# Hybrid attention and convolution layer, one core: buffer slots handed out in order of release, seven attention operations per head from VectorE to ScalarE, other operand places in the output projection, earlier residual loads

## The chip, the cores and the metric

One core of one Trainium2 chip. The time is device microseconds (us) of one launch. The engines are PE (TensorE: matmuls and transposes), DVE (VectorE), ACT (ScalarE), POOL (GpSimd) and SP (SyncE, which here only issues DMAs). Each engine runs its own instructions in program order; semaphores join them.

## The reference

One layer, 512 positions behind 16 learned meta tokens, width 2048. A root-mean-square norm, one projection into all groups, a gated linear attention group (4 heads) and a short gated convolution group (8 blocks), one output projection, a second norm and the residual:

```python
xn = rmsnorm(h, g_pre)
q, k, v, z_gla, r, hc, gate_b, gate_c, z_conv = split(xn @ w_in)
log_a = log_sigmoid(r @ w_gate_up + b_gate) / 16
o = gla_chunked(q * 128 ** -0.5, k, v, log_a)   # S_t = diag(exp(log_a)) S_{t-1} + k^T v, o_t = q_t S_t
y_gla = rmsnorm(o, g_gla_out) * silu(z_gla)
y_conv = gate_b * causal_dwconv(gate_c * hc, w_conv) * silu(z_conv)
out = h + rmsnorm(concat(y_gla, y_conv) @ w_out, g_post)
```

## The kernel before, in words

**Products.** Every fp32 matmul is made of three: operands are split into a high part (`hi`) and a low part (`lo`), and hi·hi, hi·lo and lo·hi are summed. A pair of weight tiles (a `Pair`, named after its two tiles: z2z3, k1q1, v2v3, z4z5, k2q2, v4v5, z6z7, k3q3, v6v7, then h0c0, b0s0 to b7s7) goes by a Strassen scheme of seven products P5, P1, P6, P2, P3, P7, P4 instead of eight; P2 adds into the PSUM bank of P1, P3 into that of P5. The operands of the activations stand ready split in the tiles xa, xb and xt. One product is 24 matmuls.

**What a product needs.** Its weight block comes by a DMA of 512 KB into a slot named `raw` (five slots, named by their blocks "11", "12", "21", "22"). For five of the seven products DVE first adds or subtracts two blocks in place (`add`, L188, or L219 for P7). Then `split` makes the two halves: ACT casts `whi` (L123) and DVE subtracts to `wlo` (L124), three buffers each. Two products are prepared ahead of the one that PE works on.

**What leaves a product.** `away` copies PSUM to `f` and `q` on ACT (P5 and P1: L259, L262) and combines on DVE (u, v and the destination: L264, L252, L276). f, q, u, v lie in the pool `ev`, which is opened after the pool `ini` of the start is closed and takes its memory; in `ini` lie first xr (the activations) and then rstd and tt.

**Attention between products.** The stages of each head are generators of which a few steps run after each product: decay (`decay`), scores and state (`gla_b`, `gla_c`), output (`gla_d`, `gla_e`). In `decay` of a head ACT takes the absolute value (L856), Exp (L860) and Ln (L861), each of the last two behind a load of its activation table; DVE makes min(z + b, 0) (L857), subtracts the logarithm (L862), scans (L863) and goes on with L869 to L878. `gla_c` copies the first state from PSUM on DVE (L947), `gla_d` scales the output rows on DVE (L972).

**The end.** `Whole` makes the first quarter of the output projection by plain products, `Out` the other three by the seven-product scheme, in two halves each, with the operand blocks of y (11, 21, 12, 22 and the sums S1 to S4) split into places in xa, xb and xt by `y_blocks`. In the last half (`self.end`) the order is P1, P5, P6, P3, P2, P7, P4. After P3 `rest` closes the pool of xa, opens one for the residual rows in its place, and SP loads them (4 DMAs of 1 MB, L531). Then DVE ends the rows (`finish`, L556), and SP and ACT store them (L559), 16 DMAs of 256 KB.

**Order.** The program is written in the order of the loops, and a scheduler places each engine's instructions; so an instruction can stand elsewhere on its engine than the text of the kernel has it.

## Time and profile before

| | |
|---|---|
| median of 3 runs | 829.04 us (827.64 to 830.21) |
| the profiled execution | 829.95 us |
| its span from the first to the last instruction | 827.5 us |
| PE busy | 795.5 us (96%) |
| DVE busy | 698.5 us (84%) |
| ACT busy | 428.5 us (52%) |
| POOL busy | 2.3 us |
| DMA | 98.97 MB, mean 120 GB/s |

Times below are microseconds from the start of the span unless ns is written. A row of a timeline gives an instruction's start and length, and in brackets how long its engine stood idle before it and what released it. PE's own idle time in the span is short, so every view starts from PE and asks what released each of its waits.

### The profile page before, as it was taken

Reading aid. Unit: us, or ns where it says so; the run is one execution under the profiler, and the core shown is the slowest. Engines: PE = TensorE matmul, PEld = TensorE weight load, DVE = VectorE, ACT = ScalarE, POOL = GpSimd, SP = SyncE. Lnnn points to the kernel's source line nnn. Section 1 sums busy time; section 2 is a strip of 40 time slices with the busy share of each in tenths; the row PEclk is TensorE's granted clock in tenths of the full one; section 3 lists DMA queues with packets and bytes.
Section 4 is the critical chain, followed back from the end, with each engine's and each line's share of the span. In section 5 each row is a group of like instructions: output and inputs, shape, how many; then the busy total and the mean of one; then the engine's idle time right before and its main releaser. Section 6 shows DMA issues by size and latency. Waiting matters only on the chain.

```text
span 827.5 us, 15174 instructions
## 1 busy us (share of the span) xinstructions
PE 795.5 (96%) x6364; PEld 777.6 (94%) x6364; DVE 698.5 (84%) x848; ACT 428.5 (52%) x610; POOL 2.3 (0%) x14
## 2 busy tenths in 40 slices
...
GB/s 278 229 51 68 112 128 102 78 116 132 84 96 110 179 64 81 86 229 103 103 102 103 102 105 106 120 102 122 106 111 122 181 77 75 104 101 106 101 61 346
DMA packets 34052, 98.97 MB, mean 120 GB/s; under 512 B 4064, under 2 KB 8800, under 8 KB 33344
## 3 DMA queue, kind: packets, MB, share of 16 engines
...
## 4 chain that ended last, share of the span: by engine, by line
PE 80%; DVE 10%; ACT 4%; issue 3%; DMA 2%; DVEq 0%; SPq 0%; ACTq 0%
PE out L63 5%; PE out3P L63 4%; PE out1P L63 4%; PE out2P L63 3%; PE v L63 3%; PE v6v7P L63 3%; PE k2q2P L63 2%; PE h0c0P L63 2%; PE k3q3P L63 2%; PE v2v3P L63 2%; PE b0s0P L63 2%; PE h1c1P L63 2%; PE h7c7P L63 2%; PE h6c6P L63 2%; PE h5c5P L63 2%
## 5 line engine op out<-in xcount | busy, mean ns | idle before, releaser
L123 ACT CAST whi<-raw 128x1024 fp32r<-128x1024 f32 x225 | 235.5, 1051 | 274.9 <-DVE raw L188 89.0
L124 DVE TENSOR_TENSOR wlo<-raw,whi 128x1024 fp32r<-128x1024 f32 x225 | 273.7, 1220 | 61.5 <-ACT whi L123 58.9
L188 DVE TENSOR_TENSOR raw<-raw 128x1024 f32<-128x1024 f32 x75 | 90.4, 1220 | 8.2 <-DMA raw<-in_w_t_dram 7.2
L219 DVE TENSOR_TENSOR raw<-raw 128x1024 f32<-128x1024 f32 x25 | 30.5, 1221 | 0.5
L134 ACT CAST whi<-raw 128x1024 fp32r<-128x1024 f32 (+2 forms) x13 | 10.9, 845 | 19.6 <-PE v L63 12.8
L63 PE MATMUL out<-whi,xt 128*128 128x512 f32 x64 | 20.0, 394 | 0.0
L63 PE MATMUL out2P<-whi,xt 128*128 128x256 f32 x96 | 17.4, 282 | 0.4 <-ACT whi L123 0.4
L63 PE MATMUL out3P<-whi,xt 128*128 128x256 f32 x96 | 17.4, 282 | 0.4 <-ACT whi L123 0.4
L63 PE MATMUL out1P<-whi,xt 128*128 128x256 f32 x96 | 17.3, 281 | 0.0
L63 PEld LDWEIGHTS out3P<-whi,xt 128*128 128x128 f32 x96 | 14.7, 188 | 0.6 <-ACT whi L123 0.6
L63 PEld LDWEIGHTS out2P<-whi,xt 128*128 128x128 f32 x96 | 14.7, 188 | 0.6 <-ACT whi L123 0.6
L63 PEld LDWEIGHTS out1P<-whi,xt 128*128 128x128 f32 x96 | 14.8, 188 | 0.1
L63 PEld LDWEIGHTS out<-whi,xt 128*128 128x128 f32 x64 | 12.0, 188 | 2.7
L63 PE MATMUL out3P<-wlo,xt 128*128 128x256 f32 x48 | 13.5, 281 | 0.0
L63 PE MATMUL out1P<-wlo,xt 128*128 128x256 f32 x48 | 13.5, 281 | 0.0
L63 PE MATMUL out2P<-wlo,xt 128*128 128x256 f32 x48 | 13.5, 281 | 0.0
L63 PE MATMUL out<-wlo,xt 128*128 128x512 f32 x32 | 12.6, 394 | 0.0
L135 DVE TENSOR_TENSOR wlo<-raw,whi 128x1024 fp32r<-128x1024 f32 (+2 forms) x13 | 12.5, 968 | 0.0
L593 DVE SCALAR_TENSOR_TENSOR y<-hh,wc,y 128x512 f32<-128x512 f32 x16 | 12.0, 748 | 0.2
L347 ACT ACTIVATE junk<-y 128x256 f32<-128x256 f32 x18 | 7.5, 418 | 8.7 <-DVE y L465 8.4
L658 DVE SCALAR_TENSOR_TENSOR xa<-xr,gp,xa 128x528 fp32r<-128x528 f32 x8 | 5.9, 762 | 6.9 <-ACT xa L657 6.9
L63 PE MATMUL out2P<-whi,xa 128*128 128x256 f32 x64 | 11.7, 283 | 0.0
...
## 6 DMA issues: line engine op xcount, KB each, us to landing
raw<-in_w_t_dram SPq DMA_DIRECT2D x108, 512.0 KB, 4.3
...
raw<-in_w_o_dram SPq DMA_DIRECT2D x16, 256.0 KB, 3.9
...
z<-zd SPq DMA_DIRECT2D x8, 256.0 KB, 3.0
yd<-z SPq DMA_DIRECT2D x8, 256.0 KB, 2.8
...
```

The lines of the kernel that those rows point to most:

```text
L63: nc.tensor.matmul(out_, lhsT, rhs, start=start, stop=stop, **kw)
L123: A.copy(hi, raw)
L124: V.tensor_tensor(out=lo, in0=raw, in1=hi.bitcast(F32), op=ALU.subtract)
L134: A.copy(hi[:, k, :], raw[:, k, :])
L135: V.tensor_tensor(out=lo[:, k, :], in0=raw[:, k, :], in1=hi[:, k, :].bitcast(F32), op=ALU.subtract)
L188: V.tensor_tensor(out=a, in0=a, in1=b, op=ALU.add)
L219: V.tensor_tensor(out=raw["11"], in0=raw["11"], in1=raw["22"], op=ALU.subtract)
L347: A.activation(junk, oy["src"], AF.Square, accum_out=fin["ssq"][:, t, n:n + 1])
L593: V.scalar_tensor_tensor(out=y, in0=hh[:, i:i + S], scalar=wc[:, j, i:i + 1], in1=y, op0=ALU.mult, op1=ALU.add)
L658: V.scalar_tensor_tensor(out=xt[1][:, :, xk, :], in0=src, scalar=gp[:, kt:kt + 1], in1=xt[0][:, :, xk, :].bitcast(F32), op0=ALU.mult, op1= ...
```

## The change

- **Slots.** `new_raw` takes one of five named slots from a list, and `free` puts a slot back where its last reader is written; `load_free` starts the next load of one list `loads` whenever a slot is in the list. Before, each pair loaded its own blocks and, after some products, those of the next pair.
- **Attention on ACT.** In `decay` relu(−z − b) on ACT (L874 after, with a negated bias nbg that POOL makes once) replaces DVE's min(z + b, 0); the sign goes into the next operation (L880 after, a fused multiply and subtract in place of a subtraction). Exp and Ln stand before two yields instead of after one. `gla_c`'s copy and `gla_d`'s four scalings go from DVE to ACT (L965, L990 after).
- **`ini`.** tt is allocated first, ahead of xr and rstd.
- **Operands of y.** 21 and S4 lie in the third part of xt, 11 and S1 in xa, S2 in xb.
- **The end.** `rest` runs after P5 instead of P3 of the last half; the small square root that sets up the table is written there instead of in `Whole`.

```diff
+    slots = [f"raw{i}" for i in range(5)]
+    held = {}
     def new_raw(shape=None):
-        return wp.tile(shape or [P, NB, P], F32, tag="raw", name="raw", bufs=5)
+        tag = slots.pop(0)
+        t = wp.tile(shape or [P, NB, P], F32, tag=tag, name="raw", bufs=1)
+        held[id(t)] = (t, tag)
+        return t
+    def free(t):
+        slots.append(held.pop(id(t))[1])
...
     class Pair:
-        def prepare(self, name, nxt):
-            for b in ("21", "22", "11", "12"):
-                self.load(b)
+        blocks = ("21", "22", "11", "12")
+        def prepare(self, name):
...
-            if nxt and name in ("P5", "P6", "P4"):
-                nxt.load({"P5": "21", "P6": "22", "P4": "11"}[name])
-                if name == "P4":
-                    nxt.load("12")
+            if name in ("P6", "P3", "P7", "P4"):
+                free(raw[{"P6": "21", "P3": "12", "P7": "11", "P4": "22"}[name]])
...
+    def load_free():
+        while slots and loads:
+            p, b = loads.pop(0)
+            p.load(b)
     def prepare_next():
-        n = len(ready)
-        p, name, last = line[n]
-        after = [q for q, _, _ in line[n:n + 9] if q is not p]
-        ready.append(p.prepare(name, after[0] if after else None))
+        p, name, last = line[len(ready)]
+        load_free()
+        ready.append(p.prepare(name))
+        load_free()
...
-        for b, two, s in (("11", xt, 2), ("21", xa, 0), ("12", xt, 1), ("22", xb, 0)):
+        for b, two, s in (("21", xt, 2), ("11", xa, 0), ("12", xt, 1), ("22", xb, 0)):
...
-        for name, two, s, b, c in (("S1", xb, 1, "22", "21"), ("S3", xt, 0, "21", "11"),
-                                   ("S2", xa, 1, "11", "22"), ("S4", xa, 0, "12", "11")):
+        for name, two, s, b, c in (("S1", xa, 1, "22", "21"), ("S3", xt, 0, "21", "11"),
+                                   ("S2", xb, 1, "11", "22"), ("S4", xt, 2, "12", "11")):
...
             if name == "P1":
                 A.copy(q, pt)
+                if self.end:
+                    A.activation(small.tile([P, 1], F32, name="sqrt_eps2"), epst, AF.Sqrt)
             elif name == "P5":
                 A.copy(f, pt)
+                if self.end:
+                    rest()
...
                 self.put(0, 1, pt, w, sub)
-                if self.end:
-                    rest()
...
     with tc.tile_pool(name="ini", bufs=1, reuse_waits="tile") as ini:
+        tt = ini.tile([P, NB, XHALF], F32, name="tt")
         xr = ini.tile([P, KT, L], F32, name="xr")
...
             A.activation(a[:, t], zp[:, 0:XHALF], AF.Abs, bias=bg[:, h:h + 1])
-            V.tensor_scalar(out=Bc[:, t], in0=zp[:, 0:XHALF], scalar1=bg[:, h:h + 1],
-                            scalar2=0.0, op0=ALU.add, op1=ALU.min)
-        yield
+            A.activation(Bc[:, t], zp[:, 0:XHALF], AF.Relu, bias=nbg[:, h:h + 1], scale=-1.0)
         A.activation(a, a, AF.Exp, scale=-1.0)
         A.activation(a, a, AF.Ln, bias=1.0)
-        V.tensor_tensor(out=a, in0=Bc, in1=a, op=ALU.subtract)
+        yield
+        yield
+        V.scalar_tensor_tensor(out=a, in0=Bc, scalar=-1.0, in1=a, op0=ALU.mult, op1=ALU.subtract)
...
-        V.tensor_copy(stt[:, 0, :], up[0])
+        A.copy(stt[:, 0, :], up[0])
...
         for p in range(NP):
-            V.tensor_scalar(out=on[:, p, :], in0=o[p], scalar1=ss[:, p:p + 1],
-                            scalar2=None, op0=ALU.mult)
+            A.activation(on[:, p, :], o[p], AF.Copy, scale=ss[:, p:p + 1])
```

Line numbers of the kernel after differ: `add` is L200, the subtraction for P7 L230, `whi` L124, `wlo` L125, u L273, the combination L261, Exp L875, Ln L876, the scan L881, and the table root of the end L499 (before L392).

**VectorE in z4z5.** The stretch of z4z5 before, from the second rank projection's min to the low half of P7's block; raw_1749 becomes P3's block, raw_1747 P7's:

```order
L857 TENSOR_SCALAR B_1968<-zp11_1975,bg_84 128x264
L188 TENSOR_TENSOR raw_1749<-raw_1749,raw_1747 128x1024
L264 TENSOR_TENSOR u_2009<-z4z5P6_1984,q_1959 128x256
L862 TENSOR_TENSOR esx_1969<-B_1968,esx_1969 128x528
L219 TENSOR_TENSOR raw_1747<-raw_1747,raw_1556 128x1024
L124 TENSOR_TENSOR wlo_1981<-raw_1749,whi_1980 128x1024
L863 SCALAR_TENSOR_TENSOR B_1968<-keep_96,esx_1969 128x528
L124 TENSOR_TENSOR wlo_2020<-raw_1747,whi_2019 128x1024
```

And after, where raw_1703 becomes P3's block and raw_1655 P7's:

```order
L200 TENSOR_TENSOR raw_1703<-raw_1703,raw_1655 128x1024
L1005 SCALAR_TENSOR_TENSOR z_1922<-ot01_1963,gg_86,z_1922 128x512
L230 TENSOR_TENSOR raw_1655<-raw_1655,raw_1558 128x1024
L273 TENSOR_TENSOR u_2015<-z4z5P6_1990,q_1961 128x256
L125 TENSOR_TENSOR wlo_1985<-raw_1703,whi_1984 128x1024
L880 SCALAR_TENSOR_TENSOR esx_1971<-B_1970,esx_1971 128x528
L125 TENSOR_TENSOR wlo_2021<-raw_1655,whi_2020 128x1024
L881 SCALAR_TENSOR_TENSOR B_1970<-keep_97,esx_1971 128x528
```

P7's subtraction and P3's low half stand ahead of the operation that takes the logarithm; before, they stood behind it.

**ScalarE in z4z5.** From the copy of q to the casts of P3 and P7, before (whi_1980 is P3's, whi_2019 P7's):

```order
L262 COPY q_1959<-z4z5P1_1934 128x256
L856 ACTIVATE esx_1969<-zp10_1971,bg_84 128x264
L856 ACTIVATE esx_1969<-zp11_1975,bg_84 128x264
L860 ACT_TABLE_LOAD
L860 ACTIVATE esx_1969<-esx_1969 128x528
L861 ACT_TABLE_LOAD
L861 ACTIVATE esx_1969<-esx_1969 128x528
L123 CAST whi_1980<-raw_1749 128x1024
L123 CAST whi_2019<-raw_1747 128x1024
```

And after (whi_1984 is P3's, whi_2020 P7's):

```order
L873 ACTIVATE esx_1971<-zp10_1973,bg_84 128x264
L874 ACTIVATE B_1970<-zp10_1973,nbg_85 128x264
L873 ACTIVATE esx_1971<-zp11_1977,bg_84 128x264
L874 ACTIVATE B_1970<-zp11_1977,nbg_85 128x264
L875 ACT_TABLE_LOAD
L875 ACTIVATE esx_1971<-esx_1971 128x528
L124 CAST whi_1984<-raw_1703 128x1024
L876 ACT_TABLE_LOAD
L876 ACTIVATE esx_1971<-esx_1971 128x528
L124 CAST whi_2020<-raw_1655 128x1024
```

Two Relu operations are new in the row, and P3's cast has moved from behind Ln to between Exp and Ln's table load.

**VectorE in k1q1.** From the first addition for the pair that follows (v2v3, raw_1222) to the low half of P3's block (wlo_1380), before:

```order
L188 TENSOR_TENSOR raw_1222<-raw_1222,raw_1291 128x1024
L857 TENSOR_SCALAR B_1320<-zp00_1323,bg_84 128x264
L857 TENSOR_SCALAR B_1320<-zp01_1327,bg_84 128x264
L124 TENSOR_TENSOR wlo_1339<-raw_1190,whi_1338 128x1024
L188 TENSOR_TENSOR raw_1190<-raw_1190,raw_1188 128x1024
L862 TENSOR_TENSOR esx_1321<-B_1320,esx_1321 128x528
L219 TENSOR_TENSOR raw_1188<-raw_1188,raw_1068 128x1024
L863 SCALAR_TENSOR_TENSOR B_1320<-keep_96,esx_1321 128x528
L124 TENSOR_TENSOR wlo_1380<-raw_1190,whi_1379 128x1024
```

And after (raw_1194 is the pair's that follows, wlo_1379 P3's):

```order
L200 TENSOR_TENSOR raw_1194<-raw_1194,raw_1293 128x1024
L125 TENSOR_TENSOR wlo_1338<-raw_1161,whi_1337 128x1024
L200 TENSOR_TENSOR raw_1161<-raw_1161,raw_1152 128x1024
L230 TENSOR_TENSOR raw_1152<-raw_1152,raw_1070 128x1024
L880 SCALAR_TENSOR_TENSOR esx_1323<-B_1322,esx_1323 128x528
L273 TENSOR_TENSOR u_1409<-k1q1P6_1384,q_1366 128x264
L881 SCALAR_TENSOR_TENSOR B_1322<-keep_97,esx_1323 128x528
L125 TENSOR_TENSOR wlo_1379<-raw_1161,whi_1378 128x1024
```

The two min operations have left the row, u has come into it ahead of the scan, and P3's low half is still the operation behind the scan.

**ScalarE at the start.** The first rows of ACT after, the first root of the program (L71) and the one that is written in the last part (L499):

```order
L75 DMA gp<-in_g_pre_dram 128x16
L71 ACT_TABLE_LOAD
L71 ACTIVATE sqrt_eps<-epst 128x1
L681 DMA scr<-in_w_r_dram 128x256
L499 ACTIVATE sqrt_eps_8936<-epst 128x1
L670 ACTIVATE xa_108<-xr,gp 128x2x264
```

The scheduler puts L499 where it put L392 before: behind the first root, as the fifth instruction of the engine.

## Rows read from the trace of the kernel before

**Rows 1.** Busy time of each engine in three stretches: length, then busy us and instruction count of PE, PEld, DVE, ACT and POOL, the granted clock of PE, the busy share of the DMA engines, GB/s.

```profile
95.00:365.00 270.00, 258.22 (x2077) 252.39 (x2077) 230.72 (x320) 159.74 (x242) 0.52 (x1) 0.98 0.35 111
365.00:690.00 325.00, 325.00 (x2555) 316.55 (x2554) 274.20 (x297) 152.25 (x189) 0.00 (x0) 1.00 0.35 110
690.00:810.00 120.00, 119.12 (x998) 118.26 (x998) 94.58 (x101) 57.77 (x99) 0.00 (x0) 1.00 0.33 106
```

**Rows 2.** Whom PE waited for: the product that waited, the releaser, us in total, times, the longest.

```profile
PE k1q1P L63 <- DVE wlo L124: 2.8, 2, 2.1
PE v6v7P L63 <- DVE wlo L124: 2.1, 1, 2.1
PE z2z3P L63 <- ACT q L262: 1.9, 1, 1.9
PE z4z5P L63 <- ACT whi L123: 1.6, 1, 1.6
PE v4v5P L63 <- ACT whi L123: 1.6, 1, 1.6
PE b0s0P L63 <- ACT whi L123: 1.0, 1, 1.0
```

**Rows 3.** Stretches of 2 us behind three of these waits (k1q1; z4z5, three in a row; v6v7), columns as in Rows 1.

```profile
126.00:128.00 2.00, 2.00 (x12) 2.00 (x12) 1.90 (x5) 2.00 (x4) 0.00 (x0) 0.59 0.52 193
178.00:180.00 2.00, 1.37 (x7) 1.37 (x8) 2.00 (x3) 1.98 (x4) 0.00 (x0) 0.71 0.25 29
180.00:182.00 2.00, 2.00 (x11) 2.00 (x11) 2.00 (x4) 1.80 (x3) 0.00 (x0) 0.50 0.75 248
182.00:184.00 2.00, 2.00 (x18) 2.00 (x17) 2.00 (x6) 1.01 (x2) 0.00 (x0) 0.93 0.67 180
306.00:308.00 2.00, 2.00 (x11) 2.00 (x10) 2.00 (x5) 2.00 (x4) 0.00 (x0) 0.50 0.60 229
```

**Rows 4.** The operations that move, by line, over the whole run: engine, operation, tiles, count, then duration in ns (least, median, most) and first and last start. L856 and L967 are operations of ACT of the same widths.

```profile
L857 DVE TENSOR_SCALAR B<-zp,bg x8: 481/484/486, 116.8 to 297.7; 128x264 f32<-128x264 f32 x8
L947 DVE COPY stt<-up x4: 423/424/424, 151.6 to 330.9; 128x256 f32<-128x256 f32 x4
L972 DVE TENSOR_SCALAR on<-o,ss x16: 474/476/485, 162.3 to 350.9; 128x256 f32<-128x256 f32 x16
L856 ACT ACTIVATE esx<-zp,bg x8: 473/481/486, 113.0 to 294.7; 128x264 f32<-128x264 f32 x8
L967 ACT ACTIVATE on<-o x16: 375/381/385, 158.3 to 346.4; 128x256 f32<-128x256 f32 x16
```

**Rows 5.** The casts of ACT between 100 and 350 us as a group: count, busy us, mean ns, then ACT's idle us just before them and the releasers.

```profile
L123 ACT CAST whi<-raw 128x1024 fp32r<-128x1024 f32 x70 | 73.1, 1048 | 68.0 <-DVE raw L188 29.9 <-DVE raw L219 9.0 <-DVE stt L950 6.8
```

**Rows 6.** Timelines of ACT (first row), DVE and PE in z2z3.

```profile
96.59 0.37 ACT L259 COPY f<-z2z3P 128x256 f32<-128x256 f32 x1 [5.06 <-DVE xb L772]
94.06 2.42 DVE L772 TENSOR_TENSOR xb<-xr,xb 128x1056 fp32r<-128x1056 f32 x2
99.00 1.22 DVE L124 TENSOR_TENSOR wlo<-raw,whi 128x1024 fp32r<-128x1024 f32 x1
100.59 0.28 PE L63 MATMUL z2z3P<-xb,wlo 128*128 128x256 f32 x1
```

**Rows 7.** Timeline of DVE in k1q1 and at its end: the addition that waits for a load, the scan, P3's low half, u, P7's low half.

```profile
115.62 1.23 DVE L188 TENSOR_TENSOR raw<-raw 128x1024 f32<-128x1024 f32 x1 [3.62 <-DMA raw<-in_w_t_dram]
121.72 1.25 DVE L863 TENSOR_TENSOR_SCAN B<-keep,esx 128x528 f32<-128x528 f32 x1
122.88 1.20 DVE L124 TENSOR_TENSOR wlo<-raw,whi 128x1024 fp32r<-128x1024 f32 x1
125.96 0.42 DVE L264 TENSOR_TENSOR u<-k1q1P,q 128x264 f32<-128x264 f32 x1
129.59 1.22 DVE L124 TENSOR_TENSOR wlo<-raw,whi 128x1024 fp32r<-128x1024 f32 x1
```

**Rows 8.** Timelines of ACT, DVE and PE in z4z5, in the order of the chain.

```profile
171.67 1.28 ACT L860 ACT_TABLE_LOAD   x1
175.60 0.71 DVE L862 TENSOR_TENSOR esx<-B,esx 128x528 f32<-128x528 f32 x1 [0.91 <-ACT esx L861]
177.36 1.22 DVE L124 TENSOR_TENSOR wlo<-raw,whi 128x1024 fp32r<-128x1024 f32 x1
177.53 1.04 ACT L123 CAST whi<-raw 128x1024 fp32r<-128x1024 f32 x1 [1.02 <-DVE raw L219]
178.63 0.40 PE L63 MATMUL z4z5P<-xt,whi 128*128 128x256 f32 x1 [1.57 <-ACT whi L123]
```

**Rows 9.** The end: the residual loads on SP and their landing (least, median, most), the landing of the 16 stores, the last stores on ACT's queue, two stretches of 2 us (columns as in Rows 1), and the landing of a 256 KB load elsewhere (page, KB each, median us).

```profile
L531 SPq DMA_DIRECT2D xres<-in_x_dram x4: 328/424/732, 802.3 to 803.6; - x4
DMA to landing us min/median/max: 4.9/8.3/12.3
DMA to landing us min/median/max: 3.8/4.0/6.4
L559 ACTq DMA_DIRECT2D out_dram<-y x8: 338/338/375, 811.1 to 822.7; - x8
822.00:824.00 2.00, 0.00 (x0) 0.00 (x0) 0.62 (x1) 0.00 (x0) 0.00 (x0) 0.50 1.02 386
z<-zd SPq DMA_DIRECT2D x8, 256.0 KB, 3.0
```

More of the change, by code (lines that the diff above doesn't have):

```diff
@@ L77, in hymba_kernel @@
     bg = const.tile([P, H], F32, name="bg")
+    nbg = const.tile([P, H], F32, name="nbg")
     gg = const.tile([P, 2], F32, name="gg")
@@ L144, in load_gran @@
         fill_gran(gran, w_t[TILE[name]], 8 * g, 8 * g + 8)
+        free(gran[2])
         return gran
@@ L197, in __init__ @@
                 line.append((self, name, name == ORDER[-1]))
+            loads.extend((self, b) for b in self.blocks)
         def load(self, b):
-            if b not in self.raw:
-                r = new_raw()
-                g = NB * (b in ("12", "22"))
-                i = TILE[self.na if b[0] == "1" else self.nb]
-                nc.sync.dma_start(r, w_t[i][:, g:g + NB, :])
-                self.raw[b] = r
-        def prepare(self, name, nxt):
-            for b in ("21", "22", "11", "12"):
-                self.load(b)
+            r = self.raw[b] = new_raw()
+            g = NB * (b in ("12", "22"))
+            i = TILE[self.na if b[0] == "1" else self.nb]
+            nc.sync.dma_start(r, w_t[i][:, g:g + NB, :])
+        blocks = ("21", "22", "11", "12")
+        def prepare(self, name):
             raw = self.raw
@@ L356, in __init__, with prepare @@
                 line.append((self, g, g == 7))
+                loads.append((self, g))
         def load(self, g):
-            g = {"21": 0, "22": 1, "11": 2, "12": 3}.get(g, g)
-            if g not in self.raw:
-                r = self.raw[g] = new_raw([P, 2, 2 * OW])
-                for c in range(2):
-                    nc.sync.dma_start(r[:, :, c * OW:(c + 1) * OW], w_o[c, :, 2 * g:2 * g + 2, :])
-        def prepare(self, g, nxt):
-            for n in range(min(8, g + 4)):
-                self.load(n)
+            r = self.raw[g] = new_raw([P, 2, 2 * OW])
+            for c in range(2):
+                nc.sync.dma_start(r[:, :, c * OW:(c + 1) * OW], w_o[c, :, 2 * g:2 * g + 2, :])
+        def prepare(self, g):
             two = split(self.raw[g], [P, 2, 2 * OW])
-            if g < 4:
-                self.load(g + 4)
-            else:
-                nxt.load(("12", "22", "11", "21")[g - 4])
+            free(self.raw[g])
             return two
@@ L416, in __init__, with prepare @@
                 line.append((self, n, n == "P4"))
+            loads.extend((self, b) for b in ("11", "12", "22", "21"))
         def load(self, b):
[L419 to L424 removed]
+            r = self.raw[b] = new_raw([P, 4, OW])
+            k0 = 8 * (b[0] == "2") + 4 * self.g
+            nc.sync.dma_start(r, w_o[2 * self.c + (b[1] == "2"), :, k0:k0 + 4, :])
+        def prepare(self, name):
             raw = self.raw
@@ L435, in prepare @@
             two = split(raw[{"P7": "12", "P3": "22", "P2": "21"}.get(name, "11")], [P, 4, OW])
-            if nxt and name in ("P1", "P7", "P3", "P4"):
-                nxt.load({"P1": "12", "P7": "22", "P3": "11", "P4": "21"}[name])
+            for b in () if self.end else {"P7": ("12",), "P3": ("22",), "P4": ("21", "11")}.get(
+                    name, ()):
+                free(raw[b])
             return two
```

17 lines of the change are left out of this document (8 added, 9 removed).

## The prediction

> **What bounds the kernel now.** First the stretches [rows 1]: from 365 to 690 us PE is busy in all 325 us, from 690 to 810 in 119.12 of 120. Nothing can be won there except by fewer matmuls, and the change has the same ones. From 95 to 365, where the attention of the four heads stands between the products, PE lacks 270.00 - 258.22 = 11.8 us, and DVE (230.72) is fuller than ACT (159.74). Next, whom PE waits for [rows 2]: 11.0 of it in seven waits, each for a half of a weight block that came late, or once for the copy of q. Third, what a wait costs afterwards [rows 3]: behind those in k1q1, z4z5 and v6v7 the granted clock falls to 0.50, the lower of its two levels (1.2 GHz). Behind z4z5 the three rows lack 2 x (0.29 + 0.50 + 0.07) = 1.7 us of full clock. I use that price for each of the three dips. Last the end [rows 9]: DVE and the stores, with the DMA engines full (share 1.02).
>
> **The change part by part.** All gains are in us of the profiled execution.
>
> *What DVE gives up and ACT takes.* Off DVE: 8 x 0.484 + 4 x 0.424 + 16 x 0.476 = 13.2 [rows 4]. On ACT: eight Relu, priced as the Abs of the same width (0.481), and twenty copies, priced as the squares of the same width (0.381): 3.8 + 7.6 = 11.5. Scaling with a per-row scale is in no row; between 0.381 and the 0.481 of L856, which reads a per-row bias, it is nearest to the first. The subtraction that becomes a fused operation I take as even. ACT has 68.0 us of idle time ahead of its casts there [rows 5], so the sum of 11.5 fits; what counts is which operation stands ahead of which cast. The Trainium skill (ScalarE: Activation LUTs, What ACT_TABLE_LOAD costs) gives each per-row pointer operand about 93 ns; by that the sixteen scalings would take an estimated 1.5 us more on ACT, and the sum below would stay as it is.
>
> *z4z5 and v4v5.* Before, P7's subtraction and P3's low half stand on DVE behind L862, which waits for Ln (0.91 idle); so P7's cast comes at 177.53 and PE at 178.63, 1.57 late [rows 8]. In the order after, both stand ahead of that operation, and P3's cast stands between Exp and Ln's table load. From 171.67: two Relu in pairs with Abs (0.85), table load 1.28, Exp 0.65, cast 1.04: 175.5, and 1.2 later P3's low half, 176.7; PE ran out at 178.63 - 1.57 = 177.06. Then table load, Ln and P7's cast, 178.4, and its low half, 179.6. PE reaches P7 one product after P3 began at about 176.6; a product takes 24 x 119.12 / 998 = 2.86 [rows 1], so at about 179.4: late by 0.2 at most. The wait goes, and with it its dip: 1.57 + 1.7 = 3.3 (1.6 if a short wait stays that still brings the dip). v4v5 has the same pattern and a wait of 1.6 [rows 2], for which I count no dip: 1.5 (0.5 to 1.6).
>
> *z2z3 and k1q1.* With tt ahead of xr the evacuation tiles no longer lie on what DVE reads until 96.5, so ACT's copies of f and q lose their wait of 5.06 [rows 6], and PE its 1.9 [rows 2]. What is late next is P3's low half: DVE ends it at 100.22, nothing on DVE gets shorter ahead of it, and PE used it at 100.59 [rows 6]. So a wait of some 1.6 stands there instead, and only about 0.35 is won (0 to 1.95). In k1q1 DVE waits for a load until 115.62 [rows 7]; that load stands on SP behind transfers that hang on z2z3, so it moves by the same 0.35. From there to P3's low half DVE loses the two min (0.89 for both, 0.8 with overlap) and gains u (0.42, 0.35 with overlap): 0.45 shorter. P3's half ends at 123.3 instead of 124.1. P7's half, at 129.59 before [rows 7], then has only five short operations ahead of it and ends at about 126.5. Before, PE could go on with P7 only at 130.8 and took twelve other matmuls meanwhile (by the order), 12 x 258.22 / 2077 = 1.5 [rows 1]. After: 123.3 + 2.86 + 1.5 = 127.7, or 129.0 if the dip stays. I take the dip as staying and a little lost behind it: **2.0** for z2z3 and k1q1 together (0.5 if P7's half is late again, 3.8 without the dip).
>
> *v6v7.* The same chain behind a late load, without P7's delay and without an earlier landing: 0.45 (0, or 2.1 + 1.7 = 3.8 with wait and dip gone).
>
> *Output rows on ACT.* PE's transposes of a head's output need the four scalings. On ACT they take 1.5 instead of 1.9, but can stand behind a cast of 1.05 [rows 5]. Four heads: between -1.0 each and +0.4 each; two products in hand cover nearly all of it, so -0.3 in all (-1.0 to 0.4).
>
> *The end.* The four residual loads were issued from 802.3, and the last landed 12.3 after its issue, about 815.9, among the stores, of which the last is issued at 822.7 and takes 4.0 to land (median) where a 256 KB load takes 3.0 [rows 9]. Two products earlier, at 796.6, 4 MB at the 386 GB/s of the row end by about 809, before the first stores. On SP they pass nothing, since the last weight loads stand ahead of them either way. DVE's row is unchanged. So the last store lands about 1.0 sooner (0.7 to 1.3).
>
> *Nothing won, nothing lost.* Slots in order of release: the scheduler issued each load when its slot came free before, too, and SP's row of weight loads in the steady part is the same. The root's table: the scheduler puts the little root at the start of ACT in both, so the load ahead of the last roots stays. POOL's nbg is one small operation at the start, first read in k1q1. The new places of y's operands are written while PE has work without a gap [rows 1] and DVE is free for 51 of 325 us; without that cover each of the sixteen half blocks could cost a cast, 1.05. b0s0's wait of 1.0 hangs on a buffer and stays.
>
> Sum: 3.3 + 1.5 + 2.0 + 0.45 - 0.3 + 1.0 = 7.95. The profiled execution took 829.95: 822.0. It lies 0.9 above the median of 829.04, so against the median **821.1**.
>
> **The rivals.**
>
> *A, more.* DVE's relief reaches the two late halves in k1q1 and v6v7, so that their waits are too short for a dip: 3.8 instead of 2.0 and 2.15 instead of 0.45. That is 3.5 more: 817.6. For it: 13.2 us off the fuller engine. Against: behind the late load the chain has only 0.45 less in it.
>
> *B, less.* The wait changes its place: P7's half takes over from P3's, and each pair keeps a wait and its dip. z4z5 gives 1.6, v4v5 0.5, k1q1 0.5, v6v7 0, output rows -0.6, the end 0.7: 2.7, so 826.3. For it: P7's half in z4z5 comes at 179.6 for a PE that wants it at 179.4.
>
> *C, slower: ACT becomes the bound.* Ahead of each cast ACT has 68.0 / 70 = 0.97 us idle on average [rows 5]. A pair of Relu is 0.85, four scalings are 1.5. Where more than 0.97 is put directly ahead of a cast that PE is about to need, PE waits for ACT, as it does already in z4z5, v4v5 and b0s0 [rows 2]. If half of the 11.5 shows on PE and the waits stay, 5.7 is added and only the end's 1.0 is won: 833.7. Against it: the order after moves P3's cast ahead of Ln, and two products are in hand. The Trainium skill (ScalarE: Activation LUTs, Rules for kernel authors) speaks for this rival: it would have relu, add and multiply on VectorE, for its speed per element. The trace does not bear that out at these widths, 0.481 on ACT against 0.484 on DVE [rows 4].
>
> *D, the change does not do what it says.* For the root's table and the slots the order shows this already, and they stand at nothing. If the evacuation tiles still overlap what DVE reads, 0.35 to 0.7 more is missing: 821.6.
>
> **How the numbers follow.** Forecast, with D in it: 0.63. A: 0.15. B: 0.13. C: 0.05. A cancelling of several small terms near no change: 0.04. About 0.3% (2.5 us) is what a measurement of this kernel can tell from no change. Faster by more than that, below 826.55: the forecast, A and two thirds of B, 0.86. Within it: the rest of B and the cancelling, 0.09. Slower: C, 0.05. The range runs from 816.5, just below A, to 827.0, just above B, and leaves out C and the extremes.
>
> **What would show it.** In the profile after: no ACT idle of 5 us ahead of the copy of f in z2z3, and a wait of PE for a low half there of 1 to 2 us; no wait in z4z5 and v4v5 over 0.3, and a clock of 1.00 from 178 to 184; in k1q1 and v6v7 still a wait for a low half and the dip; P7's half in k1q1 within 4 us of P3's; residual loads issued two products sooner within the last half, which with what is won before is near 790; landing of the last stores nearer to 3. PE waiting for casts in many products would be C; the wait for a scaled output row ahead of the transposes would be the sign that the -0.3 is too small. It would be wrong altogether if the scheduler's order let PE stall where it had none before, in z6z7 or k3q3 above all.

## The result and the profile after

The changed kernel takes 822.59 us (median of 4 runs, 821.12 to 823.31), the kernel before, on the same chip, 829.21 (827.64 to 830.21). The ratio is 0.992 [0.9898, 0.9941]: 6.6 us, or 0.8%, faster. The profiled execution took 823.31 with a span of 820.8, where the one of before had 829.95 and 827.5, so 6.7 us have to be found in the trace.

The first view is the list of whom PE waited for in the profile after, to be laid beside [rows 2].

```profile
PE k1q1P L63 <- DVE wlo L125: 2.1, 1, 2.1
PE tpm L933 <- DVE vt L261: 1.2, 1, 1.2
PE v6v7P L63 <- DVE wlo L125: 1.2, 1, 1.2
...
PE z2z3P L63 <- ACT whi L124: 1.0, 1, 1.0
PE b0s0P L63 <- ACT whi L124: 1.0, 1, 1.0
PE k2q2P L63 <- DVE wlo L125: 0.9, 2, 0.5
...
PE k3q3P L63 <- DVE wlo L125: 0.4, 1, 0.4
```

The waits of z4z5 and v4v5 are gone, those of z2z3, k1q1 and v6v7 are shorter, and three stand where before had none: in k2q2, ahead of the transposes of z6z7 (tpm), and in k3q3. The windows show what that is worth. They run from the first matmul of z4z5, k2q2, v4v5 and z6z7 (with k3q3) to that of the next product; columns as in [rows 1]. First the kernel before, then the kernel after:

```profile
163.90:188.60 24.70, 23.13 (x181) 22.74 (x180) 21.82 (x31) 18.13 (x24) 0.00 (x0) 0.93 0.34 107
188.60:217.00 28.40, 28.40 (x234) 27.62 (x234) 23.70 (x34) 16.16 (x30) 0.00 (x0) 1.00 0.36 112
217.00:240.40 23.40, 21.84 (x180) 21.55 (x179) 21.94 (x35) 17.42 (x25) 0.00 (x0) 1.00 0.35 111
240.40:290.10 49.70, 49.58 (x412) 48.62 (x411) 42.73 (x59) 27.36 (x42) 0.00 (x0) 1.00 0.40 129
```

```profile
160.70:181.80 21.10, 21.10 (x180) 21.08 (x179) 17.81 (x22) 16.53 (x25) 0.00 (x0) 1.00 0.39 121
181.80:212.00 30.20, 29.29 (x236) 27.91 (x235) 25.90 (x38) 18.94 (x34) 0.00 (x0) 1.00 0.34 108
212.00:233.90 21.90, 21.87 (x181) 21.49 (x180) 18.21 (x25) 18.12 (x29) 0.00 (x0) 1.00 0.37 118
233.90:285.90 52.00, 50.33 (x411) 48.59 (x410) 42.71 (x57) 30.11 (x49) 0.00 (x0) 1.00 0.37 123
```

The matmul counts are the same within two, so lengths compare. z4z5 is 3.6 shorter and at full clock. k2q2 is 1.8 longer: DVE's busy time fell by 4.0 us in z4z5 (21.82 to 17.81) and rose by 2.2 here (23.70 to 25.90), and two weight halves come late. v4v5 is 1.5 shorter, and z6z7 with k3q3 2.3 longer.

Why z4z5 lost its wait is in the timeline of ACT and DVE after, which answers to [rows 8]:

```profile
170.48 0.65 ACT L875 ACTIVATE esx<-esx 128x528 f32<-128x528 f32 x1
171.03 1.03 ACT L124 CAST whi<-raw 128x1024 fp32r<-128x1024 f32 x1
172.09 1.23 DVE L125 TENSOR_TENSOR wlo<-raw,whi 128x1024 fp32r<-128x1024 f32 x1 [1.05 <-ACT whi L124]
173.92 1.99 ACT L124 CAST whi<-raw 128x1024 fp32r<-128x1024 f32 x2
174.05 0.71 DVE L880 SCALAR_TENSOR_TENSOR esx<-B,esx 128x528 f32<-128x528 f32 x1 [0.73 <-ACT esx L876]
174.99 1.23 DVE L125 TENSOR_TENSOR wlo<-raw,whi 128x1024 fp32r<-128x1024 f32 x1 [0.24 <-ACT whi L124]
```

P3's cast stands between Exp (L875) and Ln, its low half ahead of the operation that waits for Ln (L880), and P7's low half ends at 176.2. In the profile before it was P3's low half that ended only at 178.6.

In z2z3, ACT's copy of f no longer waits 5.06 for DVE [rows 6]. In k1q1 DVE's addition behind the late load starts 1.7 sooner (113.95; before 115.62), and P7's low half follows P3's by 3.1 us where it was 6.7 [rows 7]. ACT's two copies first, then DVE in k1q1:

```profile
90.91 0.36 ACT L268 COPY f<-z2z3P 128x256 f32<-128x256 f32 x1
92.33 0.37 ACT L271 COPY q<-z2z3P 128x256 f32<-128x256 f32 x1 [1.07 <-PE z2z3P L63]
```

```profile
113.95 1.22 DVE L200 TENSOR_TENSOR raw<-raw 128x1024 f32<-128x1024 f32 x1 [2.98 <-DMA raw<-in_w_t_dram]
...
120.87 1.20 DVE L125 TENSOR_TENSOR wlo<-raw,whi 128x1024 fp32r<-128x1024 f32 x1
123.95 1.22 DVE L125 TENSOR_TENSOR wlo<-raw,whi 128x1024 fp32r<-128x1024 f32 x1
```

At the end, the residual loads are issued 11.4 us sooner and land in 4.9 to 11.0; the 16 stores then land in 2.4 to 3.3 instead of 3.8 to 6.4 [rows 9]. From the end of PE's last matmul to the end of the span it is 15.8 us instead of 16.7.

```profile
L543 SPq DMA_DIRECT2D xres<-in_x_dram x4: 327/424/712, 790.9 to 792.2; - x4
DMA to landing us min/median/max: 4.9/8.0/11.0
...
DMA to landing us min/median/max: 2.4/2.8/3.3
```

The ledger sets what was gained in each place, in us, beside the forecast. A place runs from its first product's first matmul to the first matmul of the next place:

| place | forecast | measured |
|---|---|---|
| up to z2z3 | 0 | 0.2 |
| z2z3, k1q1, v2v3 | 2.0 | 3.0 |
| z4z5 | 3.3 | 3.5 |
| k2q2, z6z7, k3q3 | -0.3 (output rows) | -4.1 |
| v4v5 | 1.5 | 1.5 |
| v6v7, with h0c0 behind it | 0.45 | 2.5 |
| b0s0 | 0 | 0.2 |
| steady part, h1c1 to b7s7 | 0 | -1.3 |
| output projection | 0 | 0.2 |
| end | 1.0 | 0.9 |
| sum | 7.95 | 6.6 |

### The profile page after: what moved, and what is told of

It is laid out like the page before. It is cut to its first block, busy times and chain, and to the rows that moved or that the text cites. A ratio compares the mean times of both kernels' runs of the same rounds, so it can differ in the third digit from the quotient of the medians.

```text
span 820.8 us, 15178 instructions
## 1 busy us (share of the span) xinstructions
PE 794.0 (97%) x6364; PEld 776.2 (95%) x6364; DVE 688.4 (84%) x820; ACT 437.6 (53%) x638; POOL 3.8 (0%) x15
## 4 chain that ended last, share of the span: by engine, by line
PE 77%; DVE 12%; DMA 4%; ACT 4%; issue 2%; SPq 0%; DVEq 0%; ACTq 0%
PE out L63 5%; PE out3P L63 4%; PE out1P L63 4%; PE out2P L63 3%; PE v L63 3%; PE v2v3P L63 3%; PE h0c0P L63 2%; PE h5c5P L63 2%; PE h2c2P L63 2%; PE h7c7P L63 2%; PE h6c6P L63 2%; PE h4c4P L63 2%; PE h3c3P L63 2%; PE h1c1P L63 2%; PE b0s0P L63 2%; PE b6s6P L63 2%
## 5 line engine op out<-in xcount | busy, mean ns | idle before, releaser
L124 ACT CAST whi<-raw 128x1024 fp32r<-128x1024 f32 x225 | 235.2, 1050 | 256.7 <-DVE raw L200 85.4
L125 DVE TENSOR_TENSOR wlo<-raw,whi 128x1024 fp32r<-128x1024 f32 x225 | 273.7, 1220 | 66.7 <-ACT whi L124 61.5
L200 DVE TENSOR_TENSOR raw<-raw 128x1024 f32<-128x1024 f32 x75 | 90.3, 1219 | 6.6 <-DMA raw<-in_w_t_dram 5.6
L230 DVE TENSOR_TENSOR raw<-raw 128x1024 f32<-128x1024 f32 x25 | 30.5, 1220 | 0.6
L63 PE MATMUL out3P<-whi,xb 128*128 128x256 f32 x64 | 11.7, 282 | 0.0
L63 PE MATMUL out2P<-whi,xb 128*128 128x256 f32 x64 | 11.6, 282 | 0.0
```

Of the source, the lines that this page charges most:

```text
L63: nc.tensor.matmul(out_, lhsT, rhs, start=start, stop=stop, **kw)
L124: A.copy(hi, raw)
L125: V.tensor_tensor(out=lo, in0=raw, in1=hi.bitcast(F32), op=ALU.subtract)
L200: V.tensor_tensor(out=a, in0=a, in1=b, op=ALU.add)
L230: V.tensor_tensor(out=raw["11"], in0=raw["11"], in1=raw["22"], op=ALU.subtract)
```

## The experiments

Every kernel was timed beside the kernel before on the same chip; ratios are to that. For the attention part one table serves all: us from each product's first matmul to the next one's, in one profiled execution of each. A dip is a stretch at the lower level of the granted clock, 0.50, behind a wait; it is counted at the 1.7 us worked out from [rows 3]. The rows of k1q1 and v2v3 compare only as a sum: in before, e4, e3 and e12 PE starts v2v3 while 22 of its instructions for k1q1 are still to come (126 instructions in the row of k1q1 and 277 in that of v2v3, elsewhere 148 and 255). v6v7 and h0c0 stand in one row for the same reason.

| | before | e4 | after | e8 | e2 | e3 | e12 | e5 | e11 |
|---|---|---|---|---|---|---|---|---|---|
| z2z3 | 22.1 | 23.5 | 21.3 | 21.3 | 21.3 | 21.3 | 21.3 | 23.6 | 21.3 |
| k1q1 | 20.9 | 18.6 | 21.8 | 19.9 | 21.8 | 19.7 | 20.4 | 20.1 | 19.6 |
| v2v3 | 34.3 | 34.8 | 31.1 | 31.8 | 31.2 | 34.0 | 33.9 | 31.8 | 31.8 |
| z4z5 | 24.7 | 24.7 | 21.1 | 21.1 | 21.2 | 21.8 | 24.7 | 21.2 | 21.2 |
| k2q2 | 28.5 | 28.4 | 30.2 | 30.2 | 30.2 | 28.8 | 28.6 | 30.2 | 30.2 |
| v4v5 | 23.4 | 23.4 | 21.9 | 21.9 | 21.5 | 21.9 | 22.6 | 21.9 | 21.5 |
| z6z7 | 28.4 | 28.4 | 29.7 | 29.7 | 29.7 | 28.9 | 28.6 | 29.7 | 29.6 |
| k3q3 | 21.2 | 21.2 | 22.4 | 22.6 | 21.3 | 22.1 | 21.2 | 21.6 | 21.2 |
| v6v7, h0c0 | 50.0 | 50.4 | 47.5 | 47.5 | 47.6 | 47.7 | 47.7 | 47.5 | 47.5 |
| sum | 253.4 | 253.4 | 247.0 | 245.9 | 245.5 | 246.3 | 248.9 | 247.6 | 243.7 |
| dips | 3 | 3 | 1 | 0 | 1 | 0 | 2 | 1 | 0 |
| sum without dips | 248.3 | 248.3 | 245.3 | 245.9 | 243.8 | 246.3 | 245.5 | 245.9 | 243.7 |

**e8: the changed kernel once more,** with no edit, to see what two executions of one kernel differ by.

> The kernel after once more, unchanged, for a second profile. If the longer step of the 258 column matmuls (120.3 against 119.2 ns before, 1.3 us in seven products) belongs to the kernel, it is 120.3 here too and the time 822.6; if it belongs to one execution, some profiles of the kernels in this call show 119.2 and some 120.3 whatever the kernel.

Measured: 821.76, ratio 0.9924 [0.9902, 0.9945]. The step of the 258-column matmuls is 120.3 ns here too, so it belongs to the kernel; e9 takes it up. In this profiled execution k1q1 has no dip. The windows around the wait, columns as in [rows 1], of the kernel after and then of e8:

```profile
122.00:124.00 2.00, 1.88 (x9) 1.88 (x10) 2.00 (x7) 1.06 (x2) 0.00 (x0) 0.60 0.42 90
124.00:126.00 2.00, 2.00 (x12) 2.00 (x11) 2.00 (x4) 1.94 (x4) 0.00 (x0) 0.55 0.46 172
```

```profile
120.00:122.00 2.00, 0.52 (x6) 0.31 (x4) 2.00 (x3) 1.97 (x4) 0.00 (x0) 1.00 0.00 0
122.00:124.00 2.00, 2.00 (x16) 2.00 (x17) 2.00 (x6) 1.27 (x3) 0.00 (x0) 1.00 0.38 106
124.00:126.00 2.00, 2.00 (x17) 1.86 (x16) 2.00 (x3) 2.00 (x4) 0.00 (x0) 1.00 0.40 156
```

One kernel, two executions: with the dip PE waited 2.1 us, without it 1.5. The length does not decide either: in e3 a wait of 2.1 in the same place brought no dip, and in e12 one of 1.6 in z4z5 did. So the sums without dips are compared, and even those differ by 0.6 between after and e8. With e1, whose edit lies behind this part, the spread is 1.3 (244.6 there, with one dip taken off).

**e4: the place of tt alone,** in the kernel before.

```diff
+        tt = ini.tile([P, NB, XHALF], F32, name="tt")
         xr = ini.tile([P, KT, L], F32, name="xr")
...
-        tt = ini.tile([P, NB, XHALF], F32, name="tt")
```

> The kernel before with tt allocated ahead of xr and nothing else. Theory: ACT's wait of 5 us ahead of the copy of f and PE's 1.9 for the copy of q in z2z3 go, a wait of about 1 us for P3's or P7's half takes their place, since DVE has no gap there; 0.5 to 1.0 us off the start of k1q1, and what follows keeps it: 0.5 to 1.2 us faster than before. Rival: the whole 1.9 is won.

Measured: 826.7, ratio 0.9998 [0.9983, 1.0013]: nothing. Whom PE waits for in e4:

```profile
PE v2v3P L63 <- ACT whi L123: 1.7, 1, 1.7
PE z2z3P L63 <- ACT whi L123: 1.6, 2, 1.0
PE z4z5P L63 <- ACT whi L123: 1.6, 1, 1.6
```

The wait for q in z2z3, 1.9 [rows 2], is gone, and two waits for casts, 1.6 together, stand there instead. In its profile the 2.3 that k1q1 wins are lost in z2z3 (which has that dip now), v2v3 and v6v7.

**e5: the attention operations alone,** in the kernel before: Relu, copy and scalings on ACT, the two yields, nbg.

```diff
-            V.tensor_scalar(out=Bc[:, t], in0=zp[:, 0:XHALF], scalar1=bg[:, h:h + 1],
-                            scalar2=0.0, op0=ALU.add, op1=ALU.min)
-        yield
+            A.activation(Bc[:, t], zp[:, 0:XHALF], AF.Relu, bias=nbg[:, h:h + 1], scale=-1.0)
...
+        yield
+        yield
...
-        V.tensor_copy(stt[:, 0, :], up[0])
+        A.copy(stt[:, 0, :], up[0])
...
+            A.activation(on[:, p, :], o[p], AF.Copy, scale=ss[:, p:p + 1])
```

> The kernel before with the attention operations on ACT and the yields moved, and nothing else. Theory: this carries most of the gain: waits in z4z5 and v4v5 go with the dip of z4z5 (5.0 us), v6v7 loses its dip (2.7), k1q1 gains 1 to 2, and the new waits in k2q2, z6z7 and k3q3 (2.5 to 2.9) are there too: 5 to 6 us faster than before. Rival: slots and tt carry a half, so 2.5 to 3.5.

Measured: 823.53, ratio 0.9937 [0.9912, 0.9963]. The attention edit alone has z4z5's 3.5, v4v5's 1.5 and the losses in k2q2 and z6z7, as after. Its profile has a span of 822.2, 5.3 less than before, as expected; the medians are only 4.0 apart.

**e12: the whole change, but all 28 operations on DVE,** where they were; nbg is gone with them, and the yields, slots, loads and operand places are the new ones.

```diff
-            A.activation(Bc[:, t], zp[:, 0:XHALF], AF.Relu, bias=nbg[:, h:h + 1], scale=-1.0)
+            V.tensor_scalar(out=Bc[:, t], in0=zp[:, 0:XHALF], scalar1=bg[:, h:h + 1],
+                            scalar2=0.0, op0=ALU.add, op1=ALU.min)
...
-        A.copy(stt[:, 0, :], up[0])
+        V.tensor_copy(stt[:, 0, :], up[0])
...
-            A.activation(on[:, p, :], o[p], AF.Copy, scale=ss[:, p:p + 1])
+            V.tensor_scalar(out=on[:, p, :], in0=o[p], scalar1=ss[:, p:p + 1],
+                            scalar2=None, op0=ALU.mult)
```

> The kernel after with all 28 attention operations back on DVE and without nbg; the moved yields, slots, tt, operand places and residual loads stay. In e2 and e3, each with a part of the operations back, the scheduler kept P7's subtraction ahead of the operation that takes the logarithm; here its order in z4z5 is that of before. Theory, that the order is what won, and the move to ACT won by changing the order: the waits of 1.6 in z4z5 and v4v5 and of 2.1 in v6v7 are back, with the dips of z4z5 and v6v7; 5 to 6 us slower than after less 1.3 for the shorter step of the 258 column matmuls, so 826 to 827. Rival, that slots, tt and yields carry the gain: within 1.5 us of after.

Measured: 822.86, ratio 0.9931 [0.9916, 0.9947], no different from after, though without nbg its steady part is 0.9 shorter. Whom PE waits for in e12:

```profile
PE z4z5P L63 <- ACT whi L123: 1.6, 1, 1.6
...
PE v4v5P L63 <- DVE wlo L124: 0.8, 1, 0.8
```

z4z5's wait is back, with its dip, and half of v4v5's; the losses in k2q2, z6z7 and k3q3 are gone. DVE's order in z4z5 is that of before: the operation that waits for Ln, then P7's subtraction.

```profile
173.24 0.71 DVE L879 TENSOR_TENSOR esx<-B,esx 128x528 f32<-128x528 f32 x1 [1.10 <-ACT esx L875]
173.87 1.22 DVE L229 TENSOR_TENSOR raw<-raw 128x1024 f32<-128x1024 f32 x1
```

In e3 (below), which has the min on DVE as well, the subtraction starts at 171.52 and that operation at 173.77, and PE's wait in z4z5 is 0.3. So the order decides this wait, not the engine that has the min; the scheduler made the other order where operations had moved to ACT. Without dips, the move wins 1.8 in z4z5, 0.7 in v4v5 and 1.0 to 1.4 in k1q1 with v2v3, and pays 1.6 in k2q2, 1.1 in z6z7 and 1.2 to 1.4 in k3q3: about nothing in all. The parts don't add: attention alone wins 2.4 (e5, without dips), everything but the move to ACT 2.8 (e12), both together 2.4 to 3.0.

**e2 and e3: one half of the move each.** e2 puts the scalings back on DVE, e3 the min and the plain subtraction. With after and e12 they make a square.

```diff
-            A.activation(on[:, p, :], o[p], AF.Copy, scale=ss[:, p:p + 1])
+            V.tensor_scalar(out=on[:, p, :], in0=o[p], scalar1=ss[:, p:p + 1],
+                            scalar2=None, op0=ALU.mult)
```

> The kernel after with the sixteen output scalings back on DVE (7.6 us on DVE, 6 us off ACT). Theory, that the order around the logarithm took the waits away and the scalings' engine matters little: within 1 us of after, PE's short waits for scaled rows ahead of the transposes (4 x 0.2 us) go, and the waits for low halves in k2q2 and k3q3 stay as they are. Rival, that it is the relief of DVE: DVE falls behind, waits for low halves in k2q2, z6z7 and k3q3 grow by 1.5 us for each of the three heads that stand there, 3 to 5 us slower than after.

```diff
-            A.activation(Bc[:, t], zp[:, 0:XHALF], AF.Relu, bias=nbg[:, h:h + 1], scale=-1.0)
+            V.tensor_scalar(out=Bc[:, t], in0=zp[:, 0:XHALF], scalar1=bg[:, h:h + 1],
+                            scalar2=0.0, op0=ALU.add, op1=ALU.min)
...
-        V.scalar_tensor_tensor(out=a, in0=Bc, scalar=-1.0, in1=a, op0=ALU.mult, op1=ALU.subtract)
+        V.tensor_tensor(out=a, in0=Bc, in1=a, op=ALU.subtract)
```

> The kernel after with min and the subtraction back on DVE in place of Relu on ACT (3.9 us on DVE, 3.8 off ACT); the yields stay moved. Theory of the order: no wait in z4z5 and v4v5 comes back, as the operation that takes the logarithm still stands behind P7's subtraction; within 1 us of after. Rival of the relief: the min lie on the chain behind the late load in k1q1 and v6v7, 0.8 us in each, so 1.6 us or more slower, with the dip in v6v7 back (1.7 more).

Measured: e2 820.07, ratio 0.9909 [0.9883, 0.9936]; e3 821.19, ratio 0.9926 [0.9898, 0.9954]. Waits of PE in e3:

```profile
PE v2v3P L63 <- ACT whi L124: 1.6, 1, 1.6
...
PE ot L1004 <- ACT on L991: 0.6, 1, 0.6
```

(Both keep the copy of stt on ACT, e12 does not.) By the sums without dips: neither half on ACT 245.5, scalings alone 246.3, Relu alone 243.8, both 245.3 and 245.9. So in these profiles the Relu on ACT wins 0.4 to 1.7 and the scalings on ACT cost 0.8 to 2.1, beside a spread of 1.3 in kernels that are alike here. The scalings' cost stands in v4v5 (21.9 against 21.5 in e2 and e11) and k3q3 (21.2 to 21.3 there; with the scalings and the Relu on ACT 21.6 to 21.8 in five executions, e5 and e7 among them, and 22.4 to 22.6 in three, so some 0.8 of it comes and goes). The times only lean that way, since the intervals overlap. With e2 the losses in k2q2 and z6z7 stay, with e3 most of them is gone: they come with the Relu and the order around it, not with the scalings.

**e6: one tag for all slots, as before.**

```diff
-        t = wp.tile(shape or [P, NB, P], F32, tag=tag, name="raw", bufs=1)
+        t = wp.tile(shape or [P, NB, P], F32, tag="raw", name="raw", bufs=5)
```

> The kernel after with the five raw slots in rotation instead of by order of release; the loads are written in the same places. Theory: SP's row of loads in the steady part is the same, so within 0.5 us of after, with at most a shift in z2z3. Rival: a load then waits for the oldest slot where another is free, DVE waits for loads in k1q1 and v6v7 grow, 1 to 3 us slower. Beside it: if the 1.1 ns longer step of the 258 column matmuls (119.2 before, 120.3 after) comes from where the slots lie, it is 119.2 here.

Measured: 822.73, ratio 0.9943 [0.9925, 0.9961]; without its one dip, in z2z3, its sum in the table's terms is 245.4. The order of release of the slots is worth nothing that can be measured, and the step of the 258-column matmuls stays at 120.3.

**e1 and e10: the end.** e1 puts the call that issues the residual loads back behind P3; e10 leaves it and gives y's operands their old places.

```diff
             elif name == "P5":
                 A.copy(f, pt)
-                if self.end:
-                    rest()
...
+                if self.end:
+                    rest()
```

> The kernel after with the four residual loads back behind P3 of the last half; nothing else differs. If the earlier loads are worth what the landing of the stores shows (median 4.0 us before, 2.8 after), the span is 0.9 us longer than after, PE's last product ends at the same place, and the stores land in about 4.0 again. Rival, that the end is DVE's pace alone: no difference, and the shorter landing comes from elsewhere.

```diff
-        for b, two, s in (("21", xt, 2), ("11", xa, 0), ("12", xt, 1), ("22", xb, 0)):
+        for b, two, s in (("11", xt, 2), ("21", xa, 0), ("12", xt, 1), ("22", xb, 0)):
...
-        for name, two, s, b, c in (("S1", xa, 1, "22", "21"), ("S3", xt, 0, "21", "11"),
-                                   ("S2", xb, 1, "11", "22"), ("S4", xt, 2, "12", "11")):
+        for name, two, s, b, c in (("S1", xb, 1, "22", "21"), ("S3", xt, 0, "21", "11"),
+                                   ("S2", xa, 1, "11", "22"), ("S4", xa, 0, "12", "11")):
```

> The kernel after with the operands of y placed as before (21 and the sums S2 and S4 in xa, 11 in xt, S1 in xb), while the residual loads are still written behind P5. Putting their line back alone (e1) moved nothing, as SP issued them when the last reader of xa was done. Theory: here P3 reads xa again, so the loads go out 8.5 us ahead of PE's end instead of 14.1, the stores land in 4 us instead of 2.8, and from PE's end to the end of the span it is 16.7 to 18 us instead of 15.8: about 1 us slower than after. Rival: 15.8 as after, so the end comes from elsewhere.

Measured: e1 822.42, ratio 0.9928 [0.9907, 0.9949]; e10 823.3, ratio 0.9934 [0.992, 0.9948]. The residual loads of e1 and what SP waits for ahead of them, then the same of e10 and the landing of its stores:

```profile
L543 SPq DMA_DIRECT2D xres<-in_x_dram x4: 328/424/789, 789.6 to 790.9; - x4
...
SPq L543 <- PE out3P L63: 14.1, 1, 14.1
```

```profile
L543 SPq DMA_DIRECT2D xres<-in_x_dram x4: 328/424/876, 797.8 to 799.1; - x4
...
SPq L543 <- PE out3P L63: 19.8, 1, 19.8
...
DMA to landing us min/median/max: 3.6/4.2/6.9
```

In e1 the loads go 14.1 us before PE's last matmul ends, and SP waits 14.1 for PE, both as in after: the line moved nothing. In e10 they go 8.5 before it, and from there to the span's end it is 16.9 us instead of 15.8. So the places of y's operands do it: the residual rows lie in memory whose last reader is a product with xa, and with the new places that product comes sooner. All profiles agree: 16.7 to 18.0 in the four with the old places (before, e4, e5, e10), 15.8 to 15.9 in the ten with the new.

**e7: the reload of z on POOL's queue,** to see whether it holds up the weight load for which k1q1 waits.

```diff
-            nc.sync.dma_start(zt[e], zd[:, 2 * h + e, :])
+            nc.gpsimd.dma_start(zt[e], zd[:, 2 * h + e, :])
```

> The kernel after with the eight reloads of z issued by POOL instead of SP, so that weight loads on SP no longer stand behind a reload that waits for its store to land (5 us on SP at 104 to 109). Theory, that k1q1's wait for a low half of 2.1 and its dip come from the late load: the load for v2v3 lands 3 to 5 us sooner, DVE's wait of 3.0 goes, PE's wait in k1q1 is under 0.5 without a dip, and v6v7's 1.2 shrinks: 3 to 5 us faster than after. Rival, that DVE's own pace sets it: DVE has no more than its 3.0 to gain and the decay chain still ends in the scan, so 1 us or less.

Measured: 820.71, ratio 0.991 [0.9889, 0.9931]. DVE's addition before the late one, the weight load, and the late addition of e7:

```profile
107.03 1.22 DVE L200 TENSOR_TENSOR raw<-raw 128x1024 f32<-128x1024 f32 x1
108.28 0.33 SPq L217 DMA_DIRECT2D raw<-in_w_t_dram  x1
112.88 1.23 DVE L200 TENSOR_TENSOR raw<-raw 128x1024 f32<-128x1024 f32 x1 [2.21 <-DMA raw<-in_w_t_dram]
```

The load now goes when DVE frees its slot (108.25), and DVE waits 2.21, against 2.98 in after and 2.38 in e8; k1q1's own wait is 1.3, against 1.5 in e8. But up to the end of v2v3 e7 is only 0.2 shorter than e8 (72.8 against 73.0), and the 1.05 between their medians is within the intervals. What is left of the wait is the slot and the landing, not the queue, and the queue is worth little.

**e9: nbg 64 bytes wide instead of 16,** so that everything placed behind it moves.

```diff
-    nbg = const.tile([P, H], F32, name="nbg")
+    nbg = const.tile([P, 16], F32, name="nbg")[:, 0:H]
```

> The kernel after with the tile of the negated bias nbg made 64 bytes wide instead of 16 in each partition, so that everything allocated behind it lies 48 bytes further on; no other instruction. All kernels so far that have nbg show 120.3 ns for a step of the 258 column matmuls, the two that don't (before, and before with tt) 119.2. Theory of the address: the step is 119.2 here, the seven h products are 0.18 us shorter each, 1.3 us in all, and the time about 821. Rival, that the step comes from the other work beside the products: 120.3 stays.

Measured: 821.9, ratio 0.9919 [0.9904, 0.9933]. Windows of 240 us in the steady part, columns as in [rows 1]: before, after, e9.

```profile
400.00:640.00 240.00, 240.00 (x2023) 240.00 (x2022) 201.85 (x225) 112.57 (x139) 0.00 (x0) 1.00 0.34 108
```

```profile
400.00:640.00 240.00, 240.00 (x2010) 239.87 (x2009) 201.92 (x224) 112.32 (x139) 0.00 (x0) 1.00 0.34 110
```

```profile
400.00:640.00 240.00, 240.00 (x2020) 239.91 (x2019) 202.65 (x225) 112.48 (x139) 0.00 (x0) 1.00 0.33 110
```

PE is full in all three, yet gets 13 matmuls fewer done in after. The step of a 258-column matmul (the length of an h product over its 168 matmuls, median of seven products) is 119.2 ns in before, e4 and e12 (no nbg), 119.3 in e9 and e11, and 120.3 in every kernel with the 16-byte nbg, e5 among them. Seven h products lose 0.18 each, 1.26 in all, the steady part's -1.3. The output projection, to the end of the last matmul, gives some of it back: 165.9 us after, 166.1 before, 166.6 in e9. So the time as a whole hardly shows it.

**e11: e2, e7 and e9 together.**

> The kernel after with nbg 64 bytes wide, the sixteen output scalings back on DVE and the reloads of z issued by POOL. If the three add: 1.3 (step of the 258 column matmuls), 0.8 to 1.4 (no waits for scaled rows), 1.1 (an earlier load in k1q1, and no dip there): 3.2 to 3.8 faster than after, about 819. If they overlap, about 820.

Measured: 819.47, ratio 0.9893 [0.9878, 0.9907]. All four runs (818.81 to 820.17) lie below all eight of after and e8 (820.96 to 823.45). It is the lowest ratio here, but its interval overlaps those of e2 and e7, and 819.47 doesn't tell whether the three add (819) or overlap (820).

## Why the prediction was right

The forecast was 821.1 us in 816.5 to 827.0, and it is 822.59. The sum was off by only 1.3 us in the span, and that is in part luck: z2z3 to v2v3 and v6v7 with h0c0 gave 3.1 more than forecast, k2q2 to k3q3 and the steady part 5.1 less.

- *z4z5 and v4v5*: right in size (3.5 and 1.5) and mechanism. P3's cast stands ahead of Ln, P7's subtraction ahead of the operation that waits for Ln, and both waits and the dip are gone. With the old order on DVE z4z5's are back (e12), and either half of the move to ACT is enough for the new order and most of the gain (e2, e3).
- *Output rows on ACT, -0.3*: the step that failed; k2q2, z6z7 and k3q3 lost 4.1, for two reasons. I priced sixteen scalings and four transposes and took two products in hand as cover. The term itself was too small. The scaling took 0.470 (16 operations), not 0.381, so 1.4 more on ACT. The Trainium skill (ScalarE: Activation LUTs, What ACT_TABLE_LOAD costs) had the price nearer: its 93 ns for a pointer operand against 89 measured. The transposes of the rows (ot) were held, v4v5 is 0.4 longer than in e2 and k3q3 0.4 to 1.4, and in the sums the scalings cost 0.8 to 2.1.
- *The larger part was in no term.* k2q2 lost 1.7 and z6z7 1.2, with the scalings back on DVE just as much (e2). The stalls in z6z7 and k3q3 that I gave as the sign of being wrong altogether came (1.2 and 0.4). It is rival B's moving wait, in another place than I put it. From the end of z4z5's scan to k2q2's first matmul DVE has 8.8 us before and 4.4 after, as PE comes sooner and the chain later; in e3 it has 7.0 and in e12 8.8. With the min on DVE (e3, e12), 1.4 to 1.6 of k2q2's loss and 0.7 to 1.1 of z6z7's are gone. That PE met DVE's backlog fits these numbers, but no run moves that distance alone, so it is a reading and not shown.

The rows of the Relu and the scaling after, by line, columns as in [rows 4]:

```profile
L874 ACT ACTIVATE B<-zp,nbg x8: 472/487/500, 112.4 to 291.3; 128x264 f32<-128x264 f32 x8
L990 ACT ACTIVATE on<-o,ss x16: 461/470/482, 159.3 to 344.1; 128x256 f32<-128x256 f32 x16
```

- *z2z3 and k1q1, 2.0*: 3.0, with v2v3. The wait in z2z3 changed its place as forecast (1.9 for q, now 1.0, for a cast), and the dip in k1q1 stayed in this execution. From the start of the late addition to the end of P3's low half it is 8.1 instead of 8.5, where 0.45 less was forecast, and P7's half follows as forecast; but the addition came 1.7 sooner, not 0.35. Without the dip, as in e8, the term is 4.3, near the 3.8 that I gave for that case.
- *v6v7, 0.45*: 2.5 with h0c0, and most of it is luck: the load that the wait hangs on landed sooner. The rows of that 512 KB load among the DMA issues, before and after (KB, then us to landing):

```profile
raw<-in_w_t_dram SPq DMA_DIRECT2D x1, 512.0 KB, 5.2
```

```profile
raw<-in_w_t_dram SPq DMA_DIRECT2D x1, 512.0 KB, 3.9
```

  The wait is 1.2 with the short landing and 2.1 with the long one. e9 and e10, with the same code there as after, had 5.3 and a wait of 2.1, and e9, with the dip as well, took 49.8 in this place, 0.2 less than before. The packets show what differs. A packet of 16 KB on the queue that the profile calls instruction comes at about the time when the load ends. In the first 3.5 us behind the issue of the load (290.9 to 294.4) the profile before has this row, the one after has none:

```profile
q8 instruction: 1, 0.02, 1.7%
```

  In before, e9 and e10 it starts 3.0 to 3.3 us after the issue and takes 0.95, in e4 it starts at 1.2 and takes 2.3; within 0.02 us of its end the load's last packets follow, and the landing takes 5.2 to 5.6. In the ten executions with 3.7 to 3.9 it starts as the load's last packets end, to 0.1 us. So the load's end waits behind that packet or it doesn't, and kernels with the same code there differ in it; most of these 2.5 us can't be put down to the change.
- *The end, 1.0*: right in size (0.9) and in the chain (loads sooner, stores land sooner), wrong about which edit does it: the operand places that I had at nothing, not the line of the call.
- *Steady part and nbg, 0*: nbg's operation costs nothing that shows, but its 16 bytes cost 1.26 in the steady part.
- *Slots and the root's table, nothing*: the slots held (e6); nothing in the trace speaks against the second, and it was not tried alone.
- *Rivals*: A was half there, since v6v7's dip is gone in after and k1q1's in e8; but the first went with the shorter landing and the second came and went in one kernel, so neither is shown to be DVE's relief. Of B, the waits in k2q2, z6z7 and k3q3 are told above. D did not come, as ACT's copies no longer wait for DVE. C did not come: ACT is busy 18.12 of 21.9 us where it is fullest in the windows, v4v5, and PE has no wait there; its waits for casts are of 1.0 (z2z3, and b0s0 as before) and of 0.4 in out2 and out3, as before. The Trainium skill's rule for it (ScalarE: Activation LUTs, Rules for kernel authors: add, multiply and relu on VectorE) gives speed in bf16 as its reason, and the operations here are fp32. It fits the scalings, by e2's profile, and not the Relu, by e3's, as far as the spread of 1.3 lets one say.

Open: what decides whether a wait brings a dip; whether anything in the change decides that the instruction packet comes ahead of the end of v6v7's load or behind it; which of the yields and the loads sooner carries e12's 2.8.
